# Expert token rows fetched by indexed DMA and transposed, in a two-layer diffusion trunk with a mixture of experts

## The chip, the core and the metric

The kernel runs on one NeuronCore of a Trainium2 chip. The metric is the device time of one execution in microseconds (us), as the median of several runs; lower is better. TensorE is called PE, VectorE DVE, ScalarE ACT, GpSimd POOL and SyncE SP, as in the profile.

## What is computed

Two layers work on 256 latent tokens and 256 context tokens of width 1024. Each layer mixes tokens (attention, convolution and pooling side by side) and then runs a mixture of 32 experts. Only the second half matters here; its reference is

```python
def hierarchical_moe(h, w_rg, b_rg, w_re, b_re, w_gate, w_up, w_down):
    ...
    combine = jnp.sum(jax.nn.one_hot(expert_id, N_EXPERTS, dtype=jnp.float32) * top_w[..., None], 1)
    ...
    for e in range(N_EXPERTS):
        hid = jax.nn.silu(h @ w_gate[e]) * (h @ w_up[e])
        y = y + combine[:, e:e + 1] * (hid @ w_down[e])
    return y
```

Each token goes to two of the eight experts of its best group. Layer 0 has 512 tokens in its mixture, layer 1 only the 256 latent ones. All data is fp32.

## The kernel before

**Slots.** Each expert has 64 slots, filled in the order of the tokens that chose it. Two experts make a pair (128 slots, 16 pairs, `NP`), two pairs a quad (256 slots, 8 quads, index `q`). Tokens beyond 64 of an expert go into an extra pass: in layer 1 one such pass is laid between the pairs (`one_pass`, key `"v"` or `"o"`), further ones run only if needed (`further`, a branch at run time).

**One quad.** `onehot` (L1314, through `hot`, L1461) makes, on DVE, a 0/1 matrix of tokens by slots for the quad. `gather` (L1337) multiplies the tokens' rows with it on PE, which picks and turns them at once: out comes `XT`, 1024 features by 256 slots. fp32 rows are held as two parts, `h2h` and `h2l` (rounded value and remainder, from `exact`, L1140), so each block takes two products per block of 128 tokens: 4 token blocks in layer 0 (`nb`), 2 in layer 1. A quad is gathered in four parts of two feature blocks each: 16 products of 128x128 by 128x256 a part in layer 0, 8 in layer 1 (L1346). ACT and DVE move a part from PSUM to `XT`. `slots` (L1321) multiplies the one-hot matrix with a table `info` on PE (L1325), which gives each slot its token's number and weight (`iw`), and builds from it a place mask `gt` on DVE.

**One pair.** `half` (L1362) does the gate and up products of two experts in two halves of the features; `hidden` does tanh on ACT and two products on DVE; `turn` transposes on PE (L1382); `down` (L1403) does the down products; `weighted` scales the result on ACT and DVE into two parts `O`; `scatter` (L1415) adds the results back to the tokens by products with `gt` on PE (L1424), a product with the gate on DVE (L1427) and an addition on POOL (L1428).

**Order.** The order on PE is written out by hand (`manual_schedule`): between the big products of pair `i` stand the parts of the next quad's gather (`feed`), the scatters of the quad before (`scatters`), and, at the end of an odd pair, the slots of the next quad (`pair_slots`, L1606). In layer 0, part 0 stands between the second gate/up half of an even pair and its transpose, part 1 after its down products; part 2 stands at the same spot in the odd pair, part 3 ahead of its down products. The other engines follow an order that a scheduler sets from dependences and the order of the program.

**Weights.** An expert has 3 MB. All weights come in one fixed order (`plan`) by DMAs that SP issues (L186) into places of 1 MB: `pump` issues the next piece as soon as a place is free, and `done` gives a place back once PE has used it. Layer 0's experts have the six places of the ring and one more (`more_`, L1458), layer 1's twelve.

**Buffers.** `big` gives named regions of SBUF. `h2h` and `h2l` of layer 0 fill c0a, c0b, c1a and c1b; in layer 1 they fill c0a and c1a. Layer 0 keeps `XT` in two sets in turn (one in "w", one in b0b and b1b), layer 1 in one.

## Time and profile before

| | |
|---|---|
| median of 3 runs | 1098.04 us (1097.34 to 1098.76) |
| the profiled execution: own time | 1093.05 us |
| its span, first to last instruction | 1091.4 us, mean granted PE clock 0.960 |
| PE matmul busy | 990.4 us, 91% |
| DVE / ACT / POOL busy | 612.8 / 310.9 / 288.8 us |
| DMA | 296.70 MB, mean 272 GB/s |

Busy time of PE counts matmuls that overlap only once; their ends are modelled. A duration of a single matmul is longer than its share of a run of them, so the time of many is read from the start of the first to the start of what follows. Shares of the whole span mix the mixing stages (about 20 to 290 us and 630 to 800 us) with the two expert stages (about 293 to 613 us and 802 to 1072 us), which is why the rows below are cut by stage.

### The profile page before, as it was taken

Reading aid. Unit: us, or ns where it says so; the run is one execution under the profiler, and the core shown is the slowest. Engines: PE = TensorE matmul, PEld = TensorE weight load, DVE = VectorE, ACT = ScalarE, POOL = GpSimd, SP = SyncE. Lnnn points to the kernel's source line nnn. Section 1 sums busy time; section 2 is a strip of 40 time slices with the busy share of each in tenths; the row PEclk is TensorE's granted clock in tenths of the full one; section 3 lists DMA queues with packets and bytes.
Section 4 is the critical chain, followed back from the end, with each engine's and each line's share of the span. In section 5 each row is a group of like instructions: output and inputs, shape, how many; then the busy total and the mean of one; then the engine's idle time right before and its main releaser. Section 6 shows DMA issues by size and latency. Waiting matters only on the chain. (4 is left out here: it accounts for less than half of the span.)

```text
span 1091.4 us, 14922 instructions
## 1 busy us (share of the span) xinstructions
PE 990.4 (91%) x5689; PEld 609.6 (56%) x5689; DVE 612.8 (56%) x1140; ACT 310.9 (28%) x614; POOL 288.8 (26%) x250
## 2 busy tenths in 40 slices
PE   4986899999788999999999988999788999999994
PEld 3666785687544555555554477756553444544442
DVE  3599967766752243253333589887783333334335
ACT  2443455624211111111111163644231222221211
POOL 2355420003360122221313553200260111013122
PEclk9996999999799999999999989999988999999997
DMA  9952326865858998999998957448688999999951
GB/s 354 334 183 75 116 78 232 309 131 181 306 188 289 387 323 322 332 333 321 322 346 301 365 168 238 168 156 293 192 276 289 392 380 392 386 394 385 381 218 39
DMA packets 90558, 296.70 MB, mean 272 GB/s; under 512 B 7409, under 2 KB 27889, under 8 KB 82417
## 3 DMA queue, kind: packets, MB, share of 16 engines
q1 hardware_dynamic: 89744, 293.77, 75.2%
q10 hardware_dynamic: 576, 1.39, 0.4%
q0 software_dynamic: 160, 0.52, 0.3%
q8 instruction: 47, 0.77, 0.3%
q14 instruction: 31, 0.25, 0.1%
HBM read 294.09 MB, written 1.57 MB: 271 GB/s over the span
## 5 line engine op out<-in xcount | busy, mean ns | idle before, releaser
L1428 POOL TENSOR_TENSOR x<-x,tm 128x512 f32<-128x512 f32 x96 | 121.0, 1280 | 434.2 <-DVE tm L1427 433.9
L1366 PE MATMUL gu<-ring,xt 128*64 128x512 f32 x664 | 202.1, 612 | 5.1 <-DMA ring<-in_w_up_dram 5.1
L1401 DVE SCALAR_TENSOR_TENSOR O<-d,iw,O 128x512 fp32r<-128x512 f32 x63 | 47.1, 750 | 135.3 <-ACT O L1400 135.2
L1427 DVE TENSOR_TENSOR tm<-y,lnb 128x512 f32<-128x512 f32 (+1 forms) x102 | 69.0, 678 | 90.8 <-PE y L1424 89.9
L1346 PEld LDWEIGHTS x<-g,h 128*128 128x128 f32 x768 | 98.1, 194 | 33.3 <-issue 25.9
L1424 PE MATMUL y<-O,gt 128*128 128x512 f32 (+2 forms) x400 | 106.8, 403 | 4.2 <-DVE tm L1427 3.4
L1346 PE MATMUL x<-g,h 128*128 128x256 f32 x768 | 105.6, 290 | 4.7 <-DVEq L1558 1.9
L1366 PEld LDWEIGHTS gu<-ring,xt 128*64 128x64 f32 x664 | 57.6, 139 | 85.2 <-issue 79.4
L1424 PEld LDWEIGHTS y<-O,gt 128*128 128x128 f32 (+1 forms) x400 | 69.6, 188 | 46.3 <-issue 25.9
L1410 PE MATMUL d<-ring,ht 128*64 128x512 f32 x328 | 94.4, 596 | 0.0
L1366 PE MATMUL gu<-slot,xt 128*64 128x512 f32 x256 | 92.3, 604 | 0.0
L1400 ACT ACTIVATE O<-d,iw 128x512 fp32r<-128x512 f32 x63 | 43.3, 688 | 140.8 <-PE d L1410 139.2
L394 ACT ACTIVATE w<-ring 128x1024 fp32r<-128x1024 f32 (+2 forms) x50 | 47.3, 945 | 94.8 <-PE p L408 65.9
L605 DVE SCALAR_TENSOR_TENSOR c0b<-c0a,hw,c0b 128x256 f32<-128x256 f32 (+1 forms) x105 | 72.9, 741 | 0.5
L1375 DVE SCALAR_TENSOR_TENSOR hd<-th,gu 128x256 f32<-128x256 f32 x32 | 13.5, 421 | 90.4 <-ACT th L1374 90.4
L400 DVE TENSOR_TENSOR w<-ring,w 128x1024 fp32r<-128x1024 f32 (+2 forms) x40 | 50.1, 1256 | 21.0 <-ACT w L394 20.8
L407 PE MATMUL p<-w,hT 128*128 128x288 f32 (+1 forms) x112 | 38.4, 343 | 19.4 <-DVE w L400 19.4
L1410 PEld LDWEIGHTS d<-ring,ht 128*64 128x64 f32 x328 | 28.1, 137 | 44.5 <-issue 42.3
L295 PE MATMUL p<-ring,scw 128*32 128x256 f32 x672 | 46.7, 415 | 1.8 <-DMA ring<-in_w_ada_dram 1.8
L1374 ACT ACTIVATE th<-gu 128x256 f32<-128x256 f32 x32 | 12.3, 384 | 124.6 <-PE gu L1366 124.6
L1366 PEld LDWEIGHTS gu<-slot,xt 128*64 128x64 f32 x256 | 26.2, 138 | 31.4 <-issue 29.3
L407 PE MATMUL p<-w,mix 128*128 128x512 f32 x96 | 38.3, 399 | 5.5 <-DVE w L400 5.5
(421 smaller groups left out, 1838.6 us busy)
## 6 DMA issues: line engine op xcount, KB each, us to landing
ring<-in_w_ada_dram SPq DMA_DIRECT2D x46, 1024.0 KB, 7.4
ring<-in_w_gate_dram SPq DMA_DIRECT2D x83, 512.0 KB, 7.7
ring<-in_w_up_dram SPq DMA_DIRECT2D x83, 512.0 KB, 8.8
ring<-in_w_down_dram SPq DMA_DIRECT2D x39, 1024.0 KB, 9.4
slot<-in_w_gate_dram SPq DMA_DIRECT2D x34, 512.0 KB, 11.1
slot<-in_w_up_dram SPq DMA_DIRECT2D x34, 512.0 KB, 10.9
slot<-in_w_down_dram SPq DMA_DIRECT2D x14, 1024.0 KB, 10.1
ring<-in_w_in_dram SPq DMA_DIRECT2D x6, 1024.0 KB, 7.2
```

Source lines behind the costliest of these rows:

```text
L295: T.matmul(ps[32 * q:32 * q + 32, :256], scw[:, j, 6 - 2 * k:38 - 2 * k], w[:, jj, q * 256:q * 256 + 256], start=(j == 0), stop=(j == 7), ...
L394: kept_hi.append(S.activation(h_, src, AF.Copy))
L400: ins = e.tensor_tensor(l_, src, h_.bitcast(FT), op=OP.subtract)
L407: T.matmul(ps, lh, rl, start=False, stop=False, skip_group_check=True)
L605: V.scalar_tensor_tensor(acc, tap(b, k), hw[:, b, k:k + 1], acc, op0=OP.mult, op1=OP.add)
L1346: T.matmul(ps[:, jj * 256:jj * 256 + n], h2[t][:, 128 * j:128 * j + 128], g[:, t, :n], start=(t == 0 and k == 0), stop=(t == nb - 1 and k ...
L1366: T.matmul(gu[64 * s:64 * s + 64, :].rearrange("p (g c) -> p g c", g=2), xt[h][:, j % 4, o0 + 64 * s:o0 + 64 * s + 64], ws[s].rearrange("p ...
L1401: V.scalar_tensor_tensor(ol, ps, w, oh.bitcast(FT), op0=OP.mult, op1=OP.subtract)
L1410: T.matmul(ps[64 * s:64 * s + 64, :n], ht[:, k, 64 * s:64 * s + 64], ws(s, k, c, n), start=(k == 0), stop=(k == 1), skip_group_check=True, ...
L1424: T.matmul(ps, GT[key][r, t * 128:(t + 1) * 128], O[key][k][r, c], start=(i == 0 and k == 0), stop=(i == m - 1 and k == 1))
L1427: V.tensor_tensor(tm, ps, gates[t // 2][hf][:, c0:c0 + n], op=OP.mult)
L1428: eng.tensor_tensor(x[:, t, cols], x[:, t, cols], tm, op=OP.add)
```

## The change

Each token block's modulated row `h2` is also written to a tensor in DRAM, `h2d`, by a DMA that ACT issues. Quad 0 of each layer is gathered as before. For the other seven, `slots` is split: the table product and its copy (`iw`) come one quad earlier, the place mask (`placed`) stays where it was. Column 5 of `info` now holds the token's number less 1025, so an empty slot reads 0 and, with 1024 added, an index out of bounds, which moves nothing. `fetch` turns the column into integers on DVE and has POOL issue two indirect DMAs that bring the 128 rows of each pair into `XG`; `gather` then transposes `XG`, four 128x128 blocks a part, in place of the products. The extra pass does the same with 64 rows (`fetch_v`). Parts 0 and 1 of a quad now both stand after the even pair's down products in both layers. In layer 0 b0b and b1b hold `XG`, `XT` has one set, and c0a, c0b, c1a and c1b, free after quad 0's gather, become four more weight places; in layer 1 c0a and c1a hold the rows.

```diff
--- before.py
+++ after.py
@@ -25,6 +25,7 @@
 CAP = 64
+NONE = 1024.0
 RING = 6
...
@@ -1137,6 +1138,8 @@
+            h2d = dr.tile([128 * nq, D], FT, tag=f"h2d{l}", name="h2d")
             def exact(t):
...
@@ -1145,6 +1148,7 @@
                         (G if t in PA else V).tensor_tensor(h2[:, cols], h2[:, cols], be[t // 2][hf], op=OP.add)
+                nc.scalar.dma_start(h2d[128 * t:128 * t + 128, :], h2)
                 hh, hl = (v[t].rearrange("p (j c) -> p j c", j=8) for v in (h2h, h2l))
...
@@ -1257,7 +1261,7 @@
             G.tensor_copy(info[:, :, :, 0], tokid[:, :nb, None].to_broadcast([128, nb, 16]))
-            G.tensor_copy(info[:, :, :, 5], tokid[:, :nb, None].to_broadcast([128, nb, 16]))
+            G.tensor_scalar(info[:, :, :, 5], tokid[:, :nb, None].to_broadcast([128, nb, 16]), -NONE - 1.0, None, op0=OP.add)
             G.tensor_copy(info[:, :, :, 1:3], Cp)
...
@@ -1280,10 +1284,10 @@
                             G.tensor_tensor(xs, xs, lg1_[1][hf], op=OP.add)
-        return h2h, h2l, (cA, cB), pos, cnt, C, info, dA, g_
-    def moe(l, h2h, h2l, mod, pos, cnt, C, info, dA, g_):
+        return h2h, h2l, h2d, (cA, cB), pos, cnt, C, info, dA, g_
+    def moe(l, h2h, h2l, h2d, mod, pos, cnt, C, info, dA, g_):
         last = l == L - 1
...
@@ -1302,10 +1306,10 @@
             if last:
-                XTS = [[big(b, [128, 4, 256], FT, "xt") for b in ("b0b", "b1b")]] * 2
+                XTS = [big(b, [128, 4, 256], FT, "xt") for b in ("b0b", "b1b")]
             else:
                 xt_ = big("w", [128, 8, 256], FT, "xt")
-                XTS = [[xt_[:, 0:4, :], xt_[:, 4:8, :]]]
+                XTS = [xt_[:, 0:4, :], xt_[:, 4:8, :]]
             GT, IW, XT, O, kept = {}, {}, {}, {}, {}
...
@@ -1324,23 +1328,53 @@
                 own = key == "o"
-                iw = sb.tile([128, 8], FT, tag="iwo" if own else "iw", name="iw", bufs=1 if own else 4)
+                iw = sb.tile([128, 8], FT, tag="iwo" if own else "iw", name="iw", bufs=1 if own else 6)
                 S.activation(iw[:, :6], pi[:, :6], AF.Copy)
+                IW[key] = iw
+                if own:
+                    placed(key, gt)
+            def placed(key, gt=None):
+                own, iw = key == "o", IW[key]
                 V.tensor_tensor(iw[0:64, 6:7], iw[0:64, 1:2], iw[0:64, 3:4], op=OP.add)
                 V.tensor_tensor(iw[64:128, 6:7], iw[64:128, 2:3], iw[64:128, 4:5], op=OP.add)
-                IW[key] = iw
                 if gt is None:
...
+            def fetch_v():
+                ix = sb.tile([128, 1], I32, tag="ix", name="ix", bufs=2)
+                V.tensor_scalar(ix, IW["o"][:, 5:6], NONE, None, op0=OP.add)
+                G.indirect_dma_start(out=kept["xo"], out_offset=None, in_=h2d[:, :],
+                                     in_offset=bass.IndirectOffsetOnAxis(ap=ix[0:64, 0:1], axis=0),
+                                     bounds_check=128 * nb - 1, oob_is_err=False)
+            def fetch(q):
+                for k in range(2):
+                    ix = sb.tile([128, 1], I32, tag="ix", name="ix", bufs=2)
+                    V.tensor_scalar(ix, IW[2 * q + k][:, 5:6], NONE, None, op0=OP.add)
+                    G.indirect_dma_start(out=XG[k], out_offset=None, in_=h2d[:, :],
+                                         in_offset=bass.IndirectOffsetOnAxis(ap=ix[:, 0:1], axis=0),
+                                         bounds_check=128 * nb - 1, oob_is_err=False)
             def gather(key, g, n, part):
...
                 if key != "v":
-                    XT[key] = XTS[key % 2]
+                    XT[key] = XTS
                 ps = pbank("x")
...
                     j = 2 * part + jj
+                    if g is None and key == "v":
+                        T.transpose(ps[:, 256 * jj:256 * jj + 64], kept["xo"][:, j::8], ident[0:64, 0:64])
+                        continue
+                    if g is None:
+                        for k in range(2):
+                            o = 256 * jj + 128 * k
+                            T.transpose(ps[:, o:o + 128], XG[k][:, j::8], ident)
+                        continue
                     for t in range(nb):
...
@@ -1455,8 +1489,8 @@
             if not last:
-                more_ = big("w", [128, 2048], FT, "slot")
-                slot(more_)
+                more_ = [big("w", [128, 2048], FT, "slot")]
+                slot(more_[0])
...
@@ -1502,7 +1536,7 @@
                 for k in (0, 5):
-                    V.tensor_copy(inf[:, :, k], tokid[:, :nb])
+                    V.tensor_scalar(inf[:, :, k], tokid[:, :nb], -NONE - 1.0 if k else 0.0, None, op0=OP.add)
                 for k in (1, 2):
...
@@ -1607,6 +1641,10 @@
+            def pair_places(q):
+                for k in range(2):
+                    placed(2 * q + k)
             units = []
...
@@ -1626,7 +1664,8 @@
                 def v_in():
-                    kept["go"] = pass_in(*taken)
+                    pass_in(*taken)
+                    fetch_v()
...
@@ -1648,7 +1687,7 @@
                 for k in range(4):
-                    step(VP[0] + 1 + k // 2, ("hidden", "turned")[k % 2], lambda k=k: gather("v", kept["go"], 64, k))
+                    step(VP[0] + 1 + k // 2, ("hidden", "turned")[k % 2], lambda k=k: gather("v", None, 64, k))
                     step(VP[2] + 1, ("hidden", "turned")[k % 2],
...
@@ -1660,6 +1699,7 @@
             pair_slots(0)
+            pair_places(0)
             g_ = hot(1)
...
@@ -1673,15 +1713,28 @@
                 one_pass()
+            if last:
+                XG = big("c0a", [128, 2, D], FT, "xg")
+                XG = [XG[:, k, :] for k in range(2)]
+                kept["xo"] = big("c1a", [128, D], FT, "xo")[0:64, :]
+                G.memset(kept["xo"], 0.0)
             else:
-                XTS.append([big(b, [128, 4, 256], FT, "xt") for b in ("b0b", "b1b")])
+                XG = [big(b, [128, D], FT, "xg") for b in ("b0b", "b1b")]
+                more_ += [big(c, [128, 2048], FT, "slot") for c in ("c0a", "c0b", "c1a", "c1b")]
+                for t_ in more_[1:]:
+                    slot(t_)
+            for k in range(2):
+                G.memset(XG[k], 0.0)
             ohs, ols = (blocks(b, 3, D, FR, "O") for b in ("b0d b0a", "b1d b1a"))
             order.enter_context(tc.manual_schedule(engines={mybir.EngineType.PE}))
+            pair_slots(1)
+            fetch(1)
+            g_ = hot(2)
             for i in range(NP):
...
                 if i == NP - 2 and not last:
-                    retired.append(more_)
+                    retired.extend(more_)
                 es = (2 * i, 2 * i + 1)
...
@@ -1690,14 +1743,12 @@
                         for part in parts:
-                            gather(q + 1, g_, 256, part)
+                            gather(q + 1, None, 256, part)
...
                     scatters(2 - ns)
-                elif more and not last:
-                    feed(0)
                 else:
...
@@ -1712,6 +1763,11 @@
                     feed(3)
+                    if q + 2 < NP // 2:
+                        pair_slots(q + 2)
+                        fetch(q + 2)
+                        if q + 3 < NP // 2:
+                            g_ = hot(q + 3)
                     scatters(8)
...
@@ -1721,16 +1777,11 @@
                 if not odd:
-                    if last:
-                        feed(0, 1)
-                    else:
-                        scatters(2)
-                        feed(1)
-                        scatters(2)
+                    scatters(2 * ns - 2)
+                    feed(0, 1)
+                    scatters(2 * ns - 2)
                 elif more:
-                    pair_slots(q + 1)
-                    if q + 2 < NP // 2:
-                        g_ = hot(q + 2)
+                    pair_places(q + 1)
                 if i == 0 and not last:
```

## Rows read from the trace of the kernel before

**Rows 1.** The page, busy time by engine over the whole span.
```profile
PE 990.4 (91%) x5689; PEld 609.6 (56%) x5689; DVE 612.8 (56%) x1140; ACT 310.9 (28%) x614; POOL 288.8 (26%) x250
```

**Rows 2.** Windows: length, busy PE, PEld, DVE, ACT, POOL; granted clock; DMA share, GB/s.
```profile
300.00:310.00 10.00, 10.00 (x66) 6.44 (x64) 2.19 (x7) 1.09 (x4) 5.51 (x2) 1.00 0.58 217
313.00:613.00 300.00, 291.96 (x1501) 156.48 (x1501) 115.49 (x193) 43.32 (x90) 85.57 (x66) 0.98 0.91 322
350.00:580.00 230.00, 229.02 (x1197) 127.22 (x1198) 82.33 (x149) 32.76 (x68) 58.92 (x47) 0.99 0.93 335
810.00:820.00 10.00, 6.83 (x40) 3.49 (x36) 9.30 (x20) 1.79 (x5) 9.57 (x9) 1.00 0.66 229
850.00:1040.00 190.00, 188.46 (x956) 90.94 (x954) 69.82 (x148) 40.81 (x88) 33.90 (x27) 1.00 1.01 388
1050.00:1060.00 10.00, 10.00 (x46) 4.09 (x44) 2.24 (x5) 0.77 (x2) 2.51 (x2) 1.00 0.12 38
```

**Rows 3.** Waits of PE, 313 to 613 us: total, times, longest.
```profile
PE gu L1366 <- DMA ring<-in_w_up_dram: 5.1, 1, 5.1
```

**Rows 4.** Waits of SP's DMA queue, 313 to 600 us.
```profile
SPq L186 <- PE gu L1366: 133.0, 28, 9.5
```

**Rows 5.** Waits of SP's DMA queue, 850 to 1040 us.
```profile
SPq L186 <- PE gu L1366: 21.7, 11, 4.4
SPq L186 <- DMA ring<-in_w_gate_dram: 17.1, 18, 2.0
```

**Rows 6.** The chain that ended last, layer 1: start us, us, what.
```profile
838.48 0.39 ACT th L1374
...
839.83 0.51 PE y L1382 x2
...
858.93 3.44 PE d L1410 x16
862.37 2.07 PE x L1346 x16
864.43 3.58 PE gu L1366 x16
...
917.39 0.81 PE x L1346 x8
...
1068.98 0.86 PE gu L1410 x8
```

**Rows 7.** Timeline of PE in one quad of layer 0: start us, us, instruction.
```profile
395.63 2.14 PE L1346 MATMUL x<-g,h 128*128 128x256 f32 x16
397.61 0.41 PE L1382 MATMUL y<-ident,hd 128*128 128x128 f32 x2
...
406.93 2.03 PE L1346 MATMUL x<-g,h 128*128 128x256 f32 x16
408.80 2.03 PE L1424 MATMUL y<-O,gt 128*128 128x512 f32 x8
```

**Rows 8.** Timeline of PE, the router's transposes in layer 1.
```profile
785.76 1.14 PE L1067 MATMUL p<-ident,x 128*128 128x128 f32 x8
```

**Rows 9.** DMA queues, 313 to 600 us: packets, MB, share of 16 engines.
```profile
q1 hardware_dynamic: 22416, 91.92, 90.3%
```

**Rows 10.** Line 343, row loads: issue ns min/median/max; the last line, landing us.
```profile
L343 SPq DMA_DIRECT2D lnb<-in_rpack_dram x2: 378/378/379, 287.9 to 289.1; - x2
...
L343 POOL DMA_DIRECT2D lnb<-dA x2: 740/849/958, 817.9 to 818.8; - x2
...
DMA to landing us min/median/max: 4.9/8.5/18.0
```

**Rows 11.** Tile lnb, 700 to 860 us: landing of POOL's two DMAs.
```profile
DMA to landing us min/median/max: 5.7/6.3/6.8
```

**Rows 12.** POOL's groups: busy us, mean ns.
```profile
L420 POOL MEMSET c0a<- 128x1152 f32 x2 | 2.1, 1057 | 0.0
```

**Rows 13.** Timeline of POOL at the start of layer 0's loop.
```profile
313.51 5.68 POOL L1436 TENSOR_TENSOR x<-x,lnb 128x1024 f32<-128x1024 f32 x2 [7.78 <-DVEq L1558]
```

**Rows 14.** Timeline of PE, layer 0's last expert product.
```profile
611.16 1.89 PE L1410 MATMUL gu<-ring,ht 128*64 128x512 f32 x8
```

## The prediction

> **What bounds the kernel now.** I read the page's engine list first: TensorE (PE) is busy 91% of the span [rows 1], so work taken off PE is worth time wherever PE is also the last to finish. Whether it is, I asked stage by stage [rows 2]. The change touches the two MoE stages only. In layer 0 (313 to 613 us) PE works 292 of 300 us while the weight stream runs at 335 GB/s and 0.93 of the DMA engines' time. In layer 1 (850 to 1040) PE works 188.5 of 190 us, and here the stream is full too: 388 GB/s at a share of 1.01. So layer 0 hangs on PE with the stream as a near second, and layer 1 is a tie. The waits say who leads. In layer 0 PE waits for a weight only once, 5.1 us [rows 3], while SP, which issues the weights, waits 133 us for PE to give back places [rows 4]. In layer 1 SP's waits for PE fall to 21.7 us; most of the rest are for earlier DMAs [rows 5]. And the stream ends early there: from 1050 to 1060 its share is 0.12, yet PE takes the last weights only at 1068.98 [rows 2, 6]. That is a cover of some 18 us between landing and use at the end of layer 1.
>
> **The change, part by part.** *Products removed, transposes added.* Sixteen gather products cost 1.98 us from start to start (395.63 to 397.61), or 1.87 (406.93 to 408.80) [rows 7]: 0.120 us each. Layer 0 loses 7 quads x 64 = 448 of them, 53.9 us. In layer 1 sixteen cost 2.07 on the chain [rows 6], so 7 x 32 = 224 cost 29.0. The extra pass loses 32 narrow ones at 0.81 per eight [rows 6], 3.2 us. What comes instead has a twin in the trace: transposes of a 128x128 fp32 block read at a stride of 8 (L1067), eight in 1.14 us [rows 8], 0.14 each. Each layer gets 7 x 16 = 112, 15.7 us, and the pass 8, 1.1 us. Net on PE: 38.2 us in layer 0, 13.3 + 2.1 in layer 1; 53.6 in all.
>
> *A filler is lost.* The products of part 2 stand on PE between the gate/up product of an odd pair and its transpose, and cover tanh on ACT and two DVE products: 838.48 to 839.83, 1.35 us [rows 6]. In layer 0 nothing else stands there, and four transposes cover 0.56. So PE waits 0.8 us in each of 7 odd pairs, 5.5 us given back. In layer 1 a scatter still stands beside them (0.9 us), and on even pairs scatters do: nothing there.
>
> *Four more places.* Layer 0 runs on 7 places of 1 MB and gets 11 once the first gather is done. They let SP issue 4 MB at about 313 us, when the stream is not full (0.58 before it, [rows 2]). The 5.1 us wait at 351 goes; what is late next is the stream itself. Its bound: the SP queue moved 91.9 MB from 313 to 600 [rows 9], 2.1 of them for the next stage. With the rows (at most 1024 in the layer, seven eighths of them fetched, 4 KB each: 3.7 MB) that is 93.5 MB. At layer 1's 384 GB/s per full share it takes 243 us, to 556; at layer 0's own 360 (335 / 0.93), 260 us, to 573. After the last landing come the last pair's products, some 7 us: 564 or 580.
>
> *Row copies.* ACT issues six DMAs of 512 KB. An issue of this kind takes 0.38 us on SP [rows 10]: 2.3 us on ACT ahead of its copies, which partly wait for DVE anyway; I take 1.0, bounds 0 and 2.3. In layer 0 the 2.1 MB (5.4 us of stream) run into the half-empty stretch from 300 [rows 2]: 0, at worst 5.4. In layer 1 the POOL products on x behind them must wait until x is read out: 0 to 2.
>
> *Fetches.* No indirect DMA is in this trace. The nearest rows are POOL's own two DMAs of 256 KB: 0.85 us of issue each, 6.3 us to landing [rows 10, 11]. So from the slots' product: ACT and DVE 0.5, issues 1.7, landing 6.3, about 9 us. The rows of a quad are asked for before the down product of the odd pair and needed after that of the next even pair: down 3.4, gate/up 3.6, scatter 2, transpose 0.4, gate/up 3.6, down 3.4 [rows 6, 7], 16 us in layer 1; with a second scatter 18 in layer 0. Hidden, with 7 us to spare. Behind the fetch on POOL stand only scatter adds of the next pair, none of which is due in that window. Three fetches have less room. In layer 0 the first follows two memsets (1.06 each [rows 12]) from 313.5 and is needed at 326.6, but POOL's residual products (5.7 us for the first two [rows 13], as much again behind them) may stand ahead: I take 2 us, bounds 0 and 12. In layer 1 the first has about as much room as it needs: 0 to 3, at a time when the cover absorbs it. The pass's fetch is issued after pair 5 and needed 5.6 us on, so it misses by 3 us (0 to 6).
>
> *Moved.* The slots' products, one-hot masks and place masks are as many as before, DVE gains 16 index operations of 0.2 us: nothing, since DVE is busy under two fifths of these stages [rows 2].
>
> **The sum.** Layer 0 by PE: 38.2 + 5.1 - 5.5 - 2 = 35.8, so its last product ends at 613.05 - 35.8 = 577 [rows 14]. The stream's two bounds, 564 and 580, lie around it; I take 34, as fuller places will bring layer 0 nearer to 384 than to 360. Layer 1 by PE: 13.3 + 2.1 - 3 = 12.4. By the stream: the cover of 18 shrinks by 1.8 MB of rows (4.7 us at 388) and 1.05 MB of copies (2.7) to 10.6. I take 9, as both are near. Sum 34 + 9 - 1 = 42. The profiled execution took 1093.05 (span 1091.4), so 1051; the median of the runs, 1098.04, stands 5.0 above it: **1056**. Less than 0.2%, 2 us, can't be told from no change here.
>
> The Trainium skill (DMA: Bandwidth & Descriptors, Specifications) lists about 358 GB/s as the HBM limit per core. Layer 1's 388 [rows 2] is above it, so here the trace decides; by 358 layer 0's stream would end at 581, its gain would be 32 and the sum 1058.
>
> **Rivals.** *The stream takes over in layer 0.* If more places do not raise its rate and it stays at 335 as it ran, 93.5 MB last until 592, the layer until 599: 14 us gained. Layer 1, with the same added bytes, would gain 2: 15 in all, **1083**. For it: shares of 0.93 leave little room. Against: 388 at a share of 1.01 in layer 1, and 133 us in which SP had nowhere to put a weight. 0.14.
>
> *Layer 1 gives nothing.* It is full already, and 2.85 MB of rows and copies (7.4 us) join. If its cover of 18 us is eaten piece by piece (gate/up weights land later than needed in mid-stage, PE idles), only layer 0 counts: 34 - 1 = 33, **1065**. Against: PE waits for no weight there now. 0.15.
>
> *Rows come late*, the case on the slow side. Place: PE's first transposes of each quad, in both layers, with the weights of the next pair queued behind. POOL's descriptors or the full DMA queues hold the rows back, and every us beyond 16 in layer 1 and 18 in layer 0 is paid 7 times each. Landing has taken 18.0 us at its worst for DMAs of this line [rows 10]; with issue and index work 20.6, so 4.5 and 2.5 late: 49 us paid, **1105**. It decides from about 3 us late on average (42 / 14). Against: POOL's own two landed in 6.3. 0.09.
>
> The Trainium skill (SBUF — State Buffer, Who interferes with whom) says that POOL can't write descriptors while a DVE instruction holds the port the two share, which would act as this rival does. POOL's two issues ran where DVE was busy 9.3 of 10 us [rows 2, 10] and took 0.74 and 0.96; that bears it out for little.
>
> *No effect*: the products are gone from the code for 14 of 16 quads, so only gains and losses that cancel would do it. 0.02.
>
> **Numbers.** Forecast 0.60, its own range 1042 (nothing lost at the three tight fetches, layer 1's 12.4 whole, no ACT cost, odd waits half) to 1072 (layer 0 at 360 and the first fetch 12 us late). With layer 1 at nothing (0.15) and half of the stream's case the range is 1042 to 1083. Faster 0.60 + 0.15 + 0.14 = 0.89, less 0.01; no change 0.02; slower 0.10.
>
> **What would show it.** Right: L1346 down to 96 wide products, some 230 transposes beside them; a quad of layer 0 shorter by 4.7 us ((38.2 - 5.5) / 7); PE with waits of 0.8 us for DVE at the odd transposes; the stream's rate in layer 0 at 375 or more and its share at 1.0; layer 1 with PE waits for weights in place of none. Wrong: PE's transposes waiting for the indirect DMAs by several us in every quad; layer 0's stream at a share of 1.0 and under 350 GB/s; POOL busy with issues of over 3 us.

## The result and the profile after

| | before | after |
|---|---|---|
| median | 1098.4 us (1097.34 to 1099.50, 4 runs) | 1067.93 us (1061.08 to 1073.01, 4 runs) |
| ratio | | 0.9722, 95% interval 0.9681 to 0.9764 |
| the profiled execution | 1093.05 us | 1073.01 us, span 1071.4 |

The change gains 30.5 us where 42 were forecast. The changed kernel's times also lie further apart than those of the kernel before: ten runs of it lie between 1060.3 and 1073.3. In the first four the time goes with PE's mean granted clock: 0.943 and 0.950 in the longer two (1073.01 and 1071.89), 0.954 and 0.959 in the shorter. (1.00 is the higher of the clock's two levels, 2.4 GHz, and 0.50 the lower, 1.2 GHz; a value between is a mean over both.) Its profiled execution is the slowest of these four, so the two profiles differ by 20 us only; what follows compares stages, and uses two more profiles of the changed kernel and a second one of the kernel before.

The page's engine list and the windows, to be held against [rows 1, 2] (columns as there):

```profile
PE 946.6 (88%) x5217; PEld 561.0 (52%) x5217; DVE 621.0 (58%) x1169; ACT 312.6 (29%) x614; POOL 327.0 (31%) x284
```
```profile
300.00:310.00 10.00, 8.88 (x60) 6.13 (x59) 1.84 (x4) 1.44 (x4) 3.67 (x2) 1.00 0.96 314
350.00:570.00 220.00, 210.97 (x984) 99.56 (x982) 94.81 (x175) 36.28 (x74) 81.80 (x65) 1.00 1.01 384
860.00:1020.00 160.00, 151.02 (x714) 65.60 (x712) 60.00 (x134) 36.24 (x76) 40.22 (x34) 0.98 1.01 392
1040.00:1050.00 10.00, 10.00 (x50) 4.07 (x46) 4.08 (x7) 3.14 (x6) 2.52 (x2) 1.00 0.43 94
```

PE works 43.8 us less. Layer 0's stream, 335 GB/s before, now runs at 384 and a share of 1.01. At the end of layer 1 the stream still falls off (0.43) while PE works without a gap, so there is still cover there. PE's waits from 313 to 588 us, then those from 765 to 1070 us (total, times, longest):

```profile
PE y L1416 <- DVE hd L1410: 14.7, 7, 7.2
PE y L1416 <- DMA ring<-in_w_up_dram: 1.3, 1, 1.3
PE d L1444 <- DMA ring<-in_w_down_dram: 1.0, 1, 1.0
```
```profile
PE y L1329 <- DVEq L1592: 8.2, 1, 8.2
PE x L1371 <- DMA xo<-h2d,ix: 6.1, 1, 6.1
PE y L1416 <- DVE hd L1410: 3.6, 6, 1.5
```

New are waits for the products of `hd` on DVE, for the end of the run-time branch in layer 1 (L1592, ahead of quad 1's slots) and for the pass's rows (`xo`). No quad's rows (`xg`) are waited for in this profile. The group of the row fetches and their landing (28 in the two layers):

```profile
L1359 POOL DMA_INDIRECT xg<-h2d,ix x28 | 32.9, 1175 | 51.8 <-DVE ix L1358 23.1 <-DVE iw L1340 22.6 <-issue 4.7
```
```profile
DMA to landing us min/median/max: 3.3/9.0/14.7
```

The table cuts each timeline of PE at six places: the first gather product of a layer, its first slots product, the first down product, and the end of the last one. It holds all profiles of this study (us); their edits come below.

```
                    layer 0                 between   layer 1
                    gather to   first down  layers    gather to  slots to    first down
                    first down  to last               slots      first down  to last
before              29.5        290.0       190.8      8.9       16.4        243.4
before_again        29.5        289.9       191.4     10.3       14.8        243.4
after               37.9        255.4       195.0     10.5       20.2        238.2
after_again         37.5        254.9       195.2      9.0       21.8        238.2
after_third         29.2        258.0       191.6      9.1       21.9        238.4
start_later         26.7        264.6       195.5     10.3       16.9        238.1
hd_first            29.8        256.1       194.5     10.4       20.2        238.5
ix_own              33.5        256.4       188.6      9.7       21.9        235.8
no_places           30.8        271.7       190.3      9.1       22.0        238.8
res_dve             26.7        257.8       187.8      9.6       21.9        238.8
v_early             33.6        254.1       192.6      9.0       21.8        232.8
best1               26.5        262.1       193.8      8.9       18.6        230.8
best3               30.6        253.9       189.6      9.1       16.9        232.6
```

In the three profiles of the changed kernel layer 0's loop is 32 to 35 us shorter than before. Its start and the stage between the layers are longer or as long; layer 1's start, from its first gather product to its first down product, took 25.3 and 25.1 us and takes 30.7 to 31.0. Layer 1 as a whole (gather to last down product) took 268.7 and 268.5 us and takes 268.9, 269.0 and 269.4: nothing gained, where 9 had been forecast. Since one and the same kernel has starts of layer 0 of 29.2 to 37.9 us, one profile can't show what an edit does to that start; layer 1's start and the quads of both layers repeat far more closely.

### The profile page after: what moved, and what is told of

Read it like the earlier page. It is cut to its first block, busy times and chain, and to the rows that moved or that the text cites. A ratio compares the mean times of both kernels' runs of the same rounds, so it can differ in the third digit from the quotient of the medians.

```text
span 1071.4 us, 14154 instructions
## 1 busy us (share of the span) xinstructions
PE 946.6 (88%) x5217; PEld 561.0 (52%) x5217; DVE 621.0 (58%) x1169; ACT 312.6 (29%) x614; POOL 327.0 (31%) x284
## 5 line engine op out<-in xcount | busy, mean ns | idle before, releaser
L1400 PE MATMUL gu<-ring,xt 128*64 128x512 f32 x504 | 171.7, 626 | 0.0
L1400 PE MATMUL gu<-slot,xt 128*64 128x512 f32 x416 | 132.3, 605 | 0.0
L1400 PEld LDWEIGHTS gu<-ring,xt 128*64 128x64 f32 x504 | 49.4, 143 | 67.3 <-issue 63.2
L1444 PE MATMUL d<-ring,ht 128*64 128x512 f32 x264 | 82.7, 597 | 1.0 <-DMA ring<-in_w_down_dram 1.0
L1400 PEld LDWEIGHTS gu<-slot,xt 128*64 128x64 f32 x416 | 38.3, 139 | 50.1 <-issue 47.6
L1444 PE MATMUL d<-slot,ht 128*64 128x512 f32 x168 | 52.6, 595 | 0.0
L1359 POOL DMA_INDIRECT xg<-h2d,ix x28 | 32.9, 1175 | 51.8 <-DVE ix L1358 23.1
L296 PE MATMUL p<-ring,scw 128*32 128x256 f32 x672 | 44.5, 399 | 1.9 <-DMA ring<-in_w_ada_dram 1.9
L1444 PEld LDWEIGHTS d<-ring,ht 128*64 128x64 f32 x264 | 24.2, 137 | 34.9 <-issue 32.0
```

The source lines that it names most:

```text
L296: T.matmul(ps[32 * q:32 * q + 32, :256], scw[:, j, 6 - 2 * k:38 - 2 * k], w[:, jj, q * 256:q * 256 + 256], start=(j == 0), stop=(j == 7), ...
L1400: T.matmul(gu[64 * s:64 * s + 64, :].rearrange("p (g c) -> p g c", g=2), xt[h][:, j % 4, o0 + 64 * s:o0 + 64 * s + 64], ws[s].rearrange("p ...
L1444: T.matmul(ps[64 * s:64 * s + 64, :n], ht[:, k, 64 * s:64 * s + 64], ws(s, k, c, n), start=(k == 0), stop=(k == 1), skip_group_check=True, ...
```

## The experiments

Each run builds on the changed kernel unless it says otherwise; ratios are against the kernel before on the same chip.

**The yardstick.** No edit.

> The changed kernel once more, as the yardstick for the others beside it. Its four runs lay between 1061.1 and 1073.0 us, where the kernel before had kept within 2.2 us. Theory: the spread sits where PE stops and its granted clock falls (the layers' starts, the mixing stage), so another profile shows the two expert loops at the same length (255 and 238 us) and the starts and the mixing stage different by up to 10 us. Rival: it sits in the row DMAs, and PE's waits for xg and xo differ by as much.

1068.96 us (6 runs), ratio 0.9722 (0.9690 to 0.9754). As the theory had it, the loops repeat to 0.5 us; but this profile shows the start and the stage between as long as the first did. A third profile was taken for that, with one of the kernel before:

> The changed kernel a third time. Theory (the clock's phase): the two expert loops again within 1 us of 255 and 238 us, and what differs in time lies ahead of layer 0's loop and in the mixing stage (188 to 196 us). Rival (weights or rows): the loops differ by 3 us or more.

> The kernel before once more, for a second profile of its mixing stage. Theory (the clock's phase, not the change): the granted clock of 0.50 to 0.67 for 10 us late in layer 1's mixing stage, which most profiles of the changed kernel show, is seen here too or moves about, and the time from the last down product of layer 0 to the first gather product of layer 1 differs from the first profile's 190.8 us by 2 to 5. Rival (the change's doing): the stage takes 190 to 191.5 us again with 0.83 at its lowest.

The third profile (1065.25 us) has a start of 29.2 in place of 37.5 and 191.6 between the layers; its layer 0 loop is 3.1 longer, by the rival's measure, since pair 1's down products then follow pair 0's by 18.2 us in place of 15.6: a PE that comes earlier waits 2.3 us for the rows of the first fetch. The second profile of the kernel before (1095.03 us) keeps within 0.6 us of the first between the layers, as the rival had it, and within 1.6 elsewhere, though its granted clock falls to 0.66 in two stretches of 10 us there. So the stage between the layers varies with the changed kernel (187.8 to 195.5 over all its relatives) more than with the two profiles of the kernel before. The windows of that stage, in the first profile of the kernel before and in the first and third of the changed kernel:

```profile
613.04:803.80 190.76, 165.31 (x1069) 122.94 (x1069) 157.89 (x309) 82.15 (x148) 51.21 (x44) 0.94 0.65 217
588.40:783.40 195.00, 169.17 (x1068) 126.24 (x1069) 157.91 (x308) 82.13 (x147) 51.56 (x44) 0.93 0.63 219
583.63:775.20 191.57, 164.71 (x1069) 123.95 (x1068) 157.76 (x308) 81.94 (x147) 51.55 (x44) 0.95 0.65 223
```

PE's idle time in these windows hardly differs (25.5, 25.8 and 26.9 us); its busy time does, and goes with the granted clock (the column ahead of the last two). Over all thirteen profiles, cut at the instructions themselves, PE idles 25.6 to 27.1 us in this stage and is busy for 161.5 to 169.1, the least at a mean clock of 0.97 and the most at 0.93. So what varies is how fast PE runs there, and not how long it waits; what sets the clock there is open. The variation of layer 0's start has a cause that shows. The first profile, PE, DVE and POOL around it (start us, us, instruction, idle time and what ended it):

```profile
311.33 1.54 PE L1329 MATMUL y<-info,g 128*128 128x6 f32 x8 [2.45 <-DVEq L1592]
312.79 6.46 PE L1400 MATMUL gu<-ring,xt 128*64 128x512 f32 x16
326.44 0.67 PE L1416 MATMUL y<-ident,hd 128*128 128x128 f32 x2 [7.19 <-DVE hd L1410]
327.04 6.16 PE L1400 MATMUL gu<-ring,xt 128*64 128x512 f32 x16
```
```profile
320.08 5.88 DVE L1471 TENSOR_TENSOR x<-x,lnb 128x1024 f32<-128x1024 f32 x1
325.89 0.41 DVE L1410 TENSOR_TENSOR hd<-hd,gu 128x256 f32<-128x256 f32 x1
```
```profile
320.24 2.35 POOL L1471 TENSOR_TENSOR x<-x,lnb 128x1024 f32<-128x1024 f32 x1
322.53 2.34 POOL L1470 TENSOR_TENSOR x<-x,lnb 128x1024 f32<-128x1024 f32 x1
```

And the third profile, DVE and POOL:

```profile
320.10 1.21 DVE L1471 TENSOR_TENSOR x<-x,lnb 128x1024 f32<-128x1024 f32 x1
321.23 0.41 DVE L1410 TENSOR_TENSOR hd<-hd,gu 128x256 f32<-128x256 f32 x1
321.56 5.33 DVE L1339 TENSOR_TENSOR iw<-iw 64x1 f32<-64x1 f32 x1
```
```profile
322.20 2.37 POOL L1471 TENSOR_TENSOR x<-x,lnb 128x1024 f32<-128x1024 f32 x1
324.51 2.37 POOL L1470 TENSOR_TENSOR x<-x,lnb 128x1024 f32<-128x1024 f32 x1
```

One DVE operation is held up for some 5 us beside POOL's two residual operations. In the first profile it is the residual operation that stands between the two products of `hd`, so PE waits 7.19 us; and sixteen products that take 3.65 us elsewhere take 6.46 before that wait and 6.16 behind it, where the granted clock is 0.66 (310 to 320 us) and 0.50 (325 to 330). In the third it is an addition on 64 numbers (0.15 us elsewhere), behind `hd`, and PE hardly notices.

**Where quad 1's slots stand.**

```diff
-            pair_slots(1)
-            fetch(1)
-            g_ = hot(2)
             for i in range(NP):
...
                     hd = hidden(part_half(gu, i, 1))
+                if i == 0:
+                    pair_slots(1)
+                    fetch(1)
+                    g_ = hot(2)
```

> Quad 1's slots, its fetch and quad 2's one-hot mask are put behind the second gate/up half of pair 0, so that this half no longer stands behind a product that waits for the branch to end. Theory (place on PE): layer 0 from its first gather product to its first down product falls from 37.9 to about 33 us, layer 1 from its first slots product to its first down product from 20.2 to about 16.5; 7 to 9 us in all. Rival (DVE): the second product of hd comes late in layer 0 because DVE does a residual operation between the two, whatever PE does; then layer 0 gains 0 to 2 and only layer 1's 3.8 come.

1064.67 us (6 runs), ratio 0.9703 (0.9678 to 0.9728). The interval overlaps that of the yardstick, so the time alone doesn't tell the two apart. Layer 1's start, from its first slots product, is 16.9 us, as the theory said; from the first gather product it is 27.2 in place of 30.7 to 31.0, and layer 1 keeps that gain. Layer 0's start is 26.7, shorter than the theory said; but the changed kernel without any edit had 29.2 once, so how much of it is the edit's doing isn't shown. The timeline of PE at layer 1's start, in the changed kernel and then in this run:

```profile
793.89 0.51 PE L1329 MATMUL y<-info,g 128*128 128x6 f32 x4
802.61 0.98 PE L1329 MATMUL y<-info,g 128*128 128x6 f32 x4 [8.21 <-DVEq L1592]
803.52 5.16 PE L1400 MATMUL gu<-slot,xt 128*64 128x512 f32 x16
```
```profile
793.44 0.51 PE L1329 MATMUL y<-info,g 128*128 128x6 f32 x4
793.88 3.65 PE L1400 MATMUL gu<-slot,xt 128*64 128x512 f32 x16
802.99 0.98 PE L1329 MATMUL y<-info,g 128*128 128x6 f32 x4 [5.46 <-DVEq L1592]
```

The half products (3.65 us) run while the branch is decided, as in the kernel before; in the changed kernel the new slots product stood in front of them and waited for its end. In layer 0 the loop gives back 9.7 of the 10.8 us that the start gains on the yardstick: PE waits 6.0 us for the first rows, and SP waits 6.7 us for PE at the branch (3.1 in the changed kernel), so the first weight for a new place is issued 18.1 us behind the first gather product in place of 13.9.

**DVE's order.**

```diff
-                    feed(2)
+                    with tc.issue_after(kept["last"].ins):
+                        feed(2)
...
-                    residual()
+                    with tc.issue_after(kept["last"].ins):
+                        residual()
```

> Residual operations of pair 0 and the copies of part 2 on DVE are put behind hd's second product of the same pair; PE's order stays. Theory (DVE order): PE's waits for hd ahead of the turn fall from 21.9 us (18.3 in layer 0, 3.6 in layer 1) to 8 or less, and the time by 7 to 11 us. Rival (place on PE): layer 0's start is set by the half that stands behind the branch, and the odd pairs' waits are those of tanh and hd themselves; then at most 3 us come.

1064.91 us (6 runs), ratio 0.9696 (0.9672 to 0.9720). The expectation's 18.3 us for layer 0 is the sum of both layers, 14.7 and 3.6 in the first profile (11.3 and 3.6 in the third). PE's waits for `hd` fall to 5.5 and 2.4 us, below the 8 of the theory; but the time that the theory forecast, 7 to 11 us, is not shown: the medians differ by 4 us, with intervals that overlap. Part of what the start gains comes back as waits of 3.0 us for the first rows, and pair 1's down products follow pair 0's by 21.3 us in place of 15.6. One odd pair of layer 0 on DVE, in the changed kernel and then in this run:

```profile
479.78 0.42 DVE L1409 SCALAR_TENSOR_TENSOR hd<-th,gu 128x256 f32<-128x256 f32 x1 [3.27 <-ACT th L1408]
480.12 0.68 DVE L1394 COPY xt<-x 128x512 f32<-128x512 f32 x1
480.72 0.41 DVE L1410 TENSOR_TENSOR hd<-hd,gu 128x256 f32<-128x256 f32 x1
```
```profile
473.73 0.42 DVE L1409 SCALAR_TENSOR_TENSOR hd<-th,gu 128x256 f32<-128x256 f32 x1 [3.27 <-ACT th L1408]
474.19 0.42 DVE L1410 TENSOR_TENSOR hd<-hd,gu 128x256 f32<-128x256 f32 x1
474.53 0.68 DVE L1394 COPY xt<-x 128x512 f32<-128x512 f32 x1
```

The copy of the four new transposes is ready between the two products of `hd`, and DVE takes it first. Odd pairs of layer 0 go from 21.5 to 21.0 us, those of layer 1 from 16.4 to 16.1. A quad of layer 0 then takes 34.0 in place of 34.5.

**POOL's half of the residual.** On top of the edit above:

```diff
-                    e, xs = G if t % 2 else V, x[:, t, :]
+                    e, xs = V, x[:, t, :]
```

> On top of the earlier run with DVE's order changed: all eight residual operations of pair 0 on DVE, none on POOL. Theory (two engines hold each other up): the residual operations on DVE took 1.2 us alone and up to 5.9 us beside POOL's; without POOL's each takes 1.2 to 1.3 us, POOL reaches the first fetch 2.5 us or more earlier, and PE's wait for the first rows falls from 3.0 to 1 us or less; 3 to 6 us in layer 0's start. Rival (memory or the stream): the operations on DVE keep durations over 2 us without POOL's, and pair 1 comes no earlier.

1062.97 us (4 runs), ratio 0.9706 (0.9672 to 0.9739). Without POOL's, all eight operations on DVE take 1.22 us each:

```profile
L1470 DVE TENSOR_TENSOR x<-x,lnb x4: 1216/1217/1218, 318.3 to 324.0; 128x1024 f32<-128x1024 f32 x4
L1471 DVE TENSOR_TENSOR x<-x,lnb x4: 1215/1216/1218, 320.6 to 330.5; 128x1024 f32<-128x1024 f32 x4
```

So it was the two engines side by side. The first fetch is issued at 315.66 in place of 319.86 and the start is 3.1 us shorter, but PE still waits 2.6 us for the first rows (expected: 1 or less), having come earlier itself, and layer 0's loop is 1.7 us longer. In the time the forecast 3 to 6 us don't show: the ratio is no lower than without this edit (0.9696). The Trainium skill (SBUF — State Buffer, Who interferes with whom) says that a DVE instruction with two inputs in SBUF contends with a GpSimd instruction that reads SBUF; these rows agree.

**The four places.**

```diff
-                more_ += [big(c, [128, 2048], FT, "slot") for c in ("c0a", "c0b", "c1a", "c1b")]
-                for t_ in more_[1:]:
-                    slot(t_)
```

> The changed kernel without its four more weight places in layer 0 (it has seven, as before the change). Theory (places carry layer 0): the stream falls back to about 335 to 360 GB/s between 350 and 580 us, PE waits for weights for 8 us or more in place of 2.3, and layer 0's loop from first to last down product takes 263 us or more in place of 255. Rival (places are not needed): seven places feed the shorter quads as well, PE's waits for weights stay under 4 us and the loop within 2 us of 255.

1081.84 us (4 runs), ratio 0.9864 (0.9836 to 0.9892): without the places about half of the gain is gone. PE's waits for weights in layer 0 (290 to 600 us), SP's waits from 313 to 400 that matter here, and the windows:

```profile
PE gu L1400 <- DMA ring<-in_w_up_dram: 10.9, 2, 5.5
```
```profile
SPq L187 <- PE gu L1400: 28.4, 6, 11.8
SPq L344 <- POOL x L1471: 8.8, 1, 8.8
```
```profile
310.00:320.00 10.00, 6.30 (x24) 2.41 (x24) 8.83 (x11) 0.74 (x3) 8.64 (x6) 0.83 0.25 75
320.00:330.00 10.00, 8.79 (x44) 3.57 (x44) 9.97 (x5) 1.76 (x3) 9.97 (x6) 1.00 0.65 212
330.00:340.00 10.00, 5.78 (x25) 2.06 (x24) 4.32 (x10) 1.37 (x3) 0.51 (x3) 0.99 0.59 160
350.00:570.00 220.00, 206.55 (x954) 98.77 (x952) 93.60 (x172) 35.53 (x72) 78.21 (x62) 0.98 1.00 376
```

The loop grows by 14 to 17 us, but not as the theory had it. From 350 us on the stream runs at 376 GB/s with seven places too, and the quads from pair 4 on take the same 34.5 us. What the places carry is the start: without them the stream runs at 75 to 212 GB/s for 30 us, partly because SP stands 8.8 us before a row load that waits for POOL's residual, with the weights queued behind it (no such wait in the changed kernel). The loss falls on pairs 1 and 2, whose down products come 24.9 and 21.5 us behind the pair before in place of 15.6 and 13.0.

**The pass's index buffer, and its place.**

```diff
-                ix = sb.tile([128, 1], I32, tag="ix", name="ix", bufs=2)
+                ix = sb.tile([128, 1], I32, tag="ixo", name="ixo", bufs=1)
                 V.tensor_scalar(ix, IW["o"][:, 5:6], NONE, None, op0=OP.add)
```

> The pass's index column gets a buffer of its own, in place of the two that the quads' fetches share. Theory (buffer): the pass's fetch waited for the landing of quad 4's rows, which read the two buffers; with its own it is issued about 6 us earlier, PE's wait of 6.1 us for xo falls to 2 or less, the clock behind it holds, and 6 to 9 us come. Rival (landing): rows take about as long behind the weights as they took, whenever they are asked for, so the wait keeps 4 us or more and at most 2 us come.

In the changed kernel POOL issues quad 4's two fetches and then the pass's 5.65 us later:

```profile
889.39 1.28 POOL L1359 DMA_INDIRECT xg<-h2d,ix  x1
890.98 0.99 POOL L1359 DMA_INDIRECT xg<-h2d,ix  x1 [0.30 <-issue]
897.62 0.95 POOL L1349 DMA_INDIRECT xo<-h2d,ix  x1 [5.65 <-DVE ix L1348]
```

1062.47 us (5 runs), ratio 0.9694 (0.9675 to 0.9714). The edit can only act in layer 1, whose loop is 2.4 us shorter; the rest of the difference of the medians isn't its doing. The fetch goes out 2.5 us behind the pass's slots product in place of 5.8, its rows land in 7.4 us in place of 6.3, and PE's wait is 4.0 in place of 6.1: the rival's number. So the buffer cost 2 us; for the rest the fetch is asked for too late. Asking earlier:

```diff
-                step(VP[0], "end", v_in)
+                step(VP[0] - 1, "end", v_in)
```

> The extra pass's slots and its fetch stand one pair earlier on PE (behind pair 4 in place of pair 5); the index buffers stay shared. Theory: the fetch is only asked for too late (a landing of 7 to 9 us against 5.6 us of room), so with a pair's 13 us more PE's wait for xo is 0, no clock is lost behind it, and pair 6 starts its down products 16 us behind pair 5's in place of 22.4: 6 us. Rival (the queue): what is saved there comes back as a wait of quad 4's rows, which now follow the pass's, or of another pair; the layer 1 loop keeps 236 us or more in place of 238.2.

1059.62 us (4 runs), ratio 0.9649 (0.9618 to 0.9679): alone of the single edits its interval lies below that of the yardstick. Pair 6 follows pair 5 by 13.7 us in place of 22.4. PE runs through where it had stood for 6.07 us:

```profile
890.21 2.13 PE L1458 MATMUL y<-O,gt 128*128 128x512 f32 x8
892.27 0.43 PE L1371 MATMUL x<-ident,xo 64*128 64x64 f32 x2
892.63 0.50 PE L1416 MATMUL y<-ident,hd 128*128 128x128 f32 x2
```

So the late fetch cost 8.7 us there: 6.1 of waiting, and 2.6 in which PE ran on at a granted clock of 0.72 (900 to 905 us) and 0.60 (905 to 910). Of them 3.2 come back in pairs 10 and 14 (1.7 and 1.5 longer; the granted clock is 0.91 from 947 to 967), and the layer 1 loop gains 5.4, against the rival.

**All edits together.** The edits on slots, DVE's order, index buffer and pass, and the following (`kept["fetch"]` is the last fetch issued):

```diff
-                G.memset(XG[k], 0.0)
+                V.memset(XG[k], 0.0)
...
-                    with tc.issue_after(kept["last"].ins):
+                    with tc.issue_after(kept["last"].ins), tc.issue_after(kept["fetch"].ins):
                         residual()
```

> All of the edits together: quad 1's slots behind the first half, copies and residual operations behind hd, POOL's residual operations behind the first fetch, the zeroing of the row buffers on DVE, the pass one pair earlier with its own index buffer. By the stages: layer 0's start 9 to 11 us shorter without the rows' wait giving it back (6 left of it at most 2), odd pairs 0.5 each in layer 0 and 0.3 in layer 1 (5), layer 1's start 4, the pass 6: 20 to 26 us off the profiled 1071, a median of 1043 to 1050. Rival (the stream takes over): layer 0's weights can't come earlier, so what its start gains returns as waits for weights; then a median of 1052 to 1058.

1055.61 us (5 runs), ratio 0.9624 (0.9600 to 0.9647): the rival's range. The start takes 26.5 us, but layer 0's loop 262.1, with a wait of 3.8 us for a down weight in pair 3 (0.4 to 1.0 in the changed kernel's three profiles). SP stood 6.7 us at the branch, as in the run with the slots moved. The last version takes that back in layer 0 alone, leaves POOL out of the residual, and no longer holds the residual behind the fetch:

```diff
-                    e, xs = G if t % 2 else V, x[:, t, :]
+                    e, xs = V, x[:, t, :]
...
+            if not last:
+                pair_slots(1)
+                fetch(1)
+                g_ = hot(2)
             for i in range(NP):
...
-                if i == 0:
+                if i == 0 and last:
                     pair_slots(1)
                     fetch(1)
                     g_ = hot(2)
...
-                    with tc.issue_after(kept["last"].ins), tc.issue_after(kept["fetch"].ins):
+                    with tc.issue_after(kept["last"].ins):
                         residual()
```

> As the run with all edits together, but in layer 0 quad 1's slots stay ahead of the first half (in layer 1 they move behind it), and all residual operations are on DVE. Theory (the branch holds SP): with the half ahead of the branch PE reaches the branch later, SP waits for it (6.7 us in that run) and the four places fill later, which came back as waits for weights in pairs 2 and 3. With the half behind the branch SP's wait is 3 us or less, layer 0 from its first gather to its last down product takes 285 us or less (288.7 in that run, 293.2 in the changed kernel), and the median is 1050 to 1054. Rival (the stream is full anyway): layer 0 takes 288 us or more and the median is 1055 to 1058.

1054.65 us (1047.83 to 1056.38, 5 runs), ratio 0.9629 (0.9605 to 0.9652). Layer 0 from gather to last down product is 284.5 us (30.6 + 253.9) against 288.6, in a profile that is the fastest of the five runs, and SP waits 3.1 us at the branch, both as the theory had it; the median came out 0.65 us above its range, and the two versions can't be told apart by their intervals. That the branch is the cause is not shown: this version also takes POOL's part out of the residual, and the run that moved POOL's half of the residual took the same 284.5 (26.7 + 257.8) with the same wait of 3.1. Both beat the changed kernel: their intervals lie below the 0.9690 to 0.9754 of its larger sample.

## Why the prediction was right, and where its terms were wrong

The forecast was faster, 1056 us; it came at 1067.93, inside the range. The reason held: PE set the pace of layer 0, and work taken off it came out as time. That the time fell inside the range was in part luck: layer 1's 9 us did not come at all, through two waits priced too low, while the range had its slow end from a slow stream and a late first fetch in layer 0. By its steps:

- **Products and transposes.** A quad of layer 0 was to lose 5.5 us of PE's work (38.2 over 7): PE's busy time from pair 7's down products to pair 9's went from 38.57 to 33.17, 5.4. Right. That quad before and after (columns as in [rows 2]):

```profile
464.62:503.19 38.57, 38.57 (x206) 21.40 (x205) 17.05 (x34) 5.73 (x12) 10.11 (x8) 1.00 0.94 327
454.25:488.79 34.54, 33.17 (x158) 15.92 (x157) 19.58 (x37) 5.73 (x12) 13.23 (x11) 1.00 0.99 376
```

- **The lost filler.** 0.8 us an odd pair: PE waits 1.25 there, and 0.78 once DVE's copy is moved behind `hd`. The tanh and product chain was priced right; missed was the copy of part 2, which now is ready in the middle of that chain. *Moved* put DVE at nothing since it is busy under two fifths of these stages; its share did not matter, its order did (and the index operations were 29, DVE's x1140 to x1169, not 16). "In layer 1 nothing there" was wrong for the same reason: 3.6 us in all, 0.3 an odd pair of it by the copy. With it quads gave 4.0 us in layer 0 (4.7 forecast) and 1.4 in layer 1 (1.9).
- **The places.** Costed at the 5.1 us wait that they remove; taking them out costs about 16 us by the ratios (0.9864 less 0.9722, of 1097). They carry the stream over the start, where the shorter quads then need it. Mis-sized to the safe side: what the shorter quads would lose without the places was not in the sum.
- **The stream's bounds for layer 0** were right (384 GB/s, as taken from layer 1). The lower one, and the rival *the stream takes over*, read the 335 GB/s of before as a limit; the run without the places shows 376 with seven, so 335 was what PE asked for. (In the paragraph on the HBM limit, 581 is the end of the layer; the stream would end at 574.)
- **The first fetch**, 2 us of 0 to 12. PE did not wait for those rows in the first profile, but layer 0's start grew by 8.4 us; in the third it did not grow, and PE waited 2.3 us for them. The step failed in looking only at the rows: the slots product that was moved ahead of the half waits for the branch, and DVE's order around `hd` was not followed. Layer 0 gave 26.2, 27.1 and 32.4 us in the three profiles where 34 were forecast.
- **Layer 1's start**, "0 to 3, at a time when the cover absorbs it". This failed: from the first gather product to the first down product it took 5.4 to 5.9 us more. The cover is the stream's lead; PE sets the end there, so a wait of PE at the branch is paid in full, and not even for the rows: PE waits 8.2 us ahead of quad 1's slots product. The run with the slots moved gives 3.5 to 3.8 of it back.
- **The pass's fetch**, 3 us of 0 to 6, cost 8.7. The landing was priced right: these rows landed in 6.3 us, as POOL's plain DMAs had [rows 11]. What was missed is that the fetch shares its index buffers with quad 4's fetches and so goes out 3.3 us later, and that the first products behind a wait of 6.1 us take 1.06 us in place of 0.59.
- **Layer 1's stream.** PE waits for no weight there, so the rival *layer 1 gives nothing* did not happen as written, though its time, 1065, is the nearest: layer 1 gave nothing because its start and its pass took back what the quads saved.
- **Rows come late** did not happen in any quad from quad 2 on: landings of up to 14.7 us, 9.0 in the median where 6.3 was taken, stayed within the room of 16 to 18. (By its own terms of 18.0, 1.7 and 0.5 its worst case is 20.2 us and not 20.6, so 45 us paid and not 49.)
- **ACT's issues**, 1 us: the six took 0.33 us each. The stage between the layers took 0.2 to 4.4 us more, but PE idles there for 26.0 to 27.1 us against 25.6 and 26.7, so at most 1.5 us of it can be theirs; the rest goes with PE's clock.
- **Ahead of layer 0's gather**, where the prediction has no term but the copies, a small addition of the router on DVE takes 2.57 us in place of 0.16 (see the last section), and PE waits 4.2 us for the first gather product in every profile of the changed kernel and its relatives in place of 1.6.

## What to carry to other kernels

When work is moved ahead of other work on a queue, ask what the moved instruction waits for, and not only when its own result is needed: here a product of 1 us held back 3.65 us of work that could have run during a branch. A stream's rate below its peak is a limit only if nothing asked it to wait; SP's waits for places had said so. And an index or staging buffer shared by fetches puts the landing of one into the issue of the next.

## What was not expected of the hardware

An addition on 64 numbers took 5.33 us on DVE (0.15 elsewhere): it ended with the second of two POOL operations of 2.37 us that began behind it (326.89 and 326.88). The same is seen in the router ahead of layer 0's first gather product, where the changed kernel's POOL begins an addition of 2.85 us at 290.63, just ahead of one of four numbers a partition on DVE (0.16 us in the kernel before, where POOL's had ended by then):

```profile
290.93 2.57 DVE L1247 TENSOR_TENSOR t<-t 128x4 f32<-128x4 f32 x1
```

Small DVE work beside POOL is not small when it stands in a chain.
